# A two-block fp32 model on one core: elementwise work of GpSimd moved to VectorE and ScalarE, and the modulation spread over three feed-forward stages

## The chip, the core and the metric

The kernel runs on one core of one Trainium2 chip. The time is the device time of one execution in microseconds (us). Before the change three runs gave 3841.25 us as the median (3839.11 to 3844.32). TensorE (PE in the profile) multiplies matrices, VectorE (DVE), ScalarE (ACT) and GpSimd (POOL) do the elementwise work, and SyncE (SP) issues the DMA transfers. PEld is the part of TensorE that loads stationary operands.

## The reference, cut to what matters

Two blocks of two layers each, on 512 positions and 1024 channels, all in float32.

```python
# first block, layer i = 0, 1
h = rmsnorm(x, norm_mix[i]); proj = h @ w_in[i]       # state-space scan beside causal attention
x = x + concatenate([y_ssm, y_att]) @ w_out[i]
x = x + memory_attention(rmsnorm(x, norm_mem_q[i]), rmsnorm(mem, norm_mem_kv[i]), ...)
x = x + conv_glu_ffn(rmsnorm(x, norm_ffn[i]), w_up[i], ffn_conv_w[i], ffn_conv_b[i], w_down[i])
# second block, on x and on a context of 256 positions
mod   = silu(c)     @ w_mod[i] + b_mod[i]             # 6 x 1024 numbers: shift, scale, gate, twice
mod_c = silu(c_ctx) @ w_mod[i] + b_mod[i]             # the same for the context
h  = rmsnorm_2(x, g_attn[i]) * (1 + sc1) + sh1        # layer 0: neighbourhood attention
x  = x + gt1 * (o @ w_out)                            # layer 1: sliding window, with rotary positions
x  = x + gt2 * conv_ffn(modulated x, ...)
if i == 0: ctx = ctx + gt1c * (...) ; ctx = ctx + gt2c * conv_ffn(modulated ctx, ...)
```

In layer 1 the context needs only its first shift and scale, since it is not updated there any more.

## The kernel before, in words

Activations lie transposed: channels on the 128 partitions, positions along a row, so `x` is 8 tiles of 128x512. Every float32 product runs as three matmuls on split operands: a tile is rounded by ScalarE to a high part (`hi`) and VectorE subtracts it from the tile to get the low part (`lo`). `wload` (L319) does this for weights: SP loads a tile `wr` of 128x1024 numbers, ScalarE writes `wh` (L314), and another engine writes `wl` (L331). There are 2 buffers of `wr` and 3 each of `wh` and `wl`. `lin` (L304 is its matmul) multiplies high by high, high by low and low by high for each of 8 blocks of 128 channels: 24 matmuls of 512 columns for one weight tile.

The stages follow each other: for each layer of the first block the mixer, the memory attention (`mem_attn`) and the feed-forward (`ffn1`); then for the second block the context and projections (`na_ctx`), the neighbourhood attention (`na_layer`), the feed-forward on both streams (`ffn2`, layer 0), the sliding-window layer (`swa_layer`) and the feed-forward on `x` alone (`ffn2`, layer 1). One feed-forward has 22 pairs of up tiles, in parts, each part followed by its down products into `x`; in `ffn1` the downs of a part are spread over the ups of the next one. Behind each up product of `ffn1` VectorE scales it out of PSUM (L1178), makes two convolution taps (L1183) and, per pair, a gate product (L1186) and a split (L317); in `ffn2` the taps are L2025 and L2027.

GpSimd had these parts of the work. `wload` gave it one weight remainder of three in the first block's mixers, and some later (`WPC`, `WPU`). `sumsq` (L421) made most squares (L429) and nearly all sums of squares (L433) for the norms. The modulation, a matrix-vector product, is made by `mod_steps` (L1246) without TensorE: each of 96 half-rows of weights (one 128x512 load, 256 KB) is multiplied by a broadcast vector, for `x` and for the context, and summed along the row. Six of eight such products ran on GpSimd (L1284) and were summed by ScalarE (L1262, an `accum_out`), two of eight ran on VectorE with the sum in the same instruction (L1282). The steps of layer i were called from the last loop of `mem_attn` and from `ffn1` of the same layer i. GpSimd also had one of two softmax scalings of `na_layer` (L1694), head norms (L1399) and the rotation (L1771, L1762).

Instructions are issued to each engine by a scheduler that looks at the order of the code and at the tiles' readiness; each engine then takes its own in that order, one after another. `issue_after` puts an instruction behind the last matmul issued.

Of the kernel before, what the change touches and what calls it, by code (L numbers as in the profile page):

```python
# [57 lines left out]
HP = (0,1,0)  # L58
# [200 lines left out]
class Builder:  # L259
    def __init__(self, ctx, tc, a, stop=None):  # L260
        self.tc, self.nc, self.a, self.stop = tc, tc.nc, a, stop
        self.n = 0
# [260 lines left out]
    def mixer(self, i, f, fn):  # L523
# [91 lines left out]
        def group_scan(g, conv, zs, fill):  # L615
# [58 lines left out]
            for hp in range(2):  # L674
# [12 lines left out]
        def kv_in(m):  # L687
# [376 lines left out]
    def mem_attn(self, i, f, mh, K, fn):  # L1064
# [1159 lines left out]
```

## Time and profile before

| | |
|---|---|
| median of three runs | 3841.25 us |
| the profiled execution | 3832.78 us, its span 3831.0 us |
| PE, PEld busy | 3675.2 us (96%), 3062.5 us (80%) |
| DVE, ACT, POOL busy | 2669.1 us (70%), 1842.9 us (48%), 1001.0 us (26%) |
| DMA | 354.39 MB, mean 93 GB/s |

A busy time is the union of an engine's instruction times. A busy PE is not a PE at its peak, since matmuls overlap each other and their ends are modelled; the number of matmuls in a stretch tells more. The trace places the stages (us from the start of the span): `ffn1` of layer 0 from about 690 to 1070 and of layer 1 from about 1740 to 2130; `na_ctx` to 2395, `na_layer` to 2605, `ffn2` of layer 0 to 3170, `swa_layer` to 3450, `ffn2` of layer 1 to the end.

### The profile page before, as it was taken

How to read it: one execution, taken by the hardware profiler on the slowest of the kernel's cores; microseconds unless marked ns; L12 is line 12 of the kernel's file. 1: busy time of each engine (PE TensorE's matmuls, PEld its weight loads, DVE VectorE, ACT ScalarE, POOL GpSimd, SP SyncE). 2: the span in 40 equal slices, each digit the busy share in tenths (PEclk: the TensorE clock that was granted, in tenths of full speed). 3: DMA queues.
4: the chain of work that ended last, by engine and by line, in shares of the span. 5: the costliest groups of instructions: out<-in, count | busy, mean ns of one | idle time of the engine just before them, and what ended most of it. 6: DMA issues, size and time to landing. Idle time of an engine off the chain costs nothing. (4 is left out here: it accounts for less than half of the span.)

```text
span 3831.0 us, 55553 instructions
## 1 busy us (share of the span) xinstructions
PE 3675.2 (96%) x21300; PEld 3062.5 (80%) x21300; DVE 2669.1 (70%) x4599; ACT 1842.9 (48%) x3532; POOL 1001.0 (26%) x688
## 2 busy tenths in 40 slices
PE   8999999999899999999999899899999999999999
PEld 6777788777778777887777899778888888888887
DVE  7768756889977687668998753777545547657555
ACT  5645634455555456344555454774222225554232
POOL 1223243467621121234666212321000012100000
PEclk9999999999999999999999999999999999999999
DMA  3222143344422211333444332322212212012232
GB/s 112 67 72 67 51 127 100 111 154 157 146 91 72 72 57 56 126 105 102 165 155 150 123 104 92 108 73 72 66 61 61 66 56 74 15 40 93 94 95 93
DMA packets 128714, 354.39 MB, mean 93 GB/s; under 512 B 14144, under 2 KB 26816, under 8 KB 128448
## 3 DMA queue, kind: packets, MB, share of 16 engines
q1 hardware_dynamic: 127440, 349.62, 28.6%
q8 instruction: 168, 2.75, 0.3%
q10 hardware_dynamic: 1008, 1.21, 0.1%
q14 instruction: 98, 0.80, 0.1%
HBM read 346.58 MB, written 4.19 MB: 92 GB/s over the span
## 5 line engine op out<-in xcount | busy, mean ns | idle before, releaser
L304 PE MATMUL L<-A,wh 128*128 128x512 f32 (+1 forms) x6408 | 1861.5, 375 | 19.5 <-ACT wh L314 8.8
L304 PEld LDWEIGHTS L<-A,wh 128*128 128x128 f32 x6408 | 1148.0, 189 | 241.7 <-ACT wh L314 13.1
L304 PE MATMUL L<-A,wl 128*128 128x512 f32 (+1 forms) x3204 | 1194.9, 373 | 20.4 <-DVE wl L331 19.8
L314 ACT ACTIVATE wh<-wr 128x1024 fp32r<-128x1024 f32 (+4 forms) x562 | 561.9, 1001 | 787.7 <-PE L L304 429.8
L331 DVE TENSOR_TENSOR wl<-wr,wh 128x1024 fp32r<-128x1024 f32 (+4 forms) x503 | 658.7, 1311 | 327.2 <-ACT wh L314 319.1
L304 PEld LDWEIGHTS L<-A,wl 128*128 128x128 f32 x3204 | 604.7, 189 | 137.5 <-DVE wl L331 26.3
L1284 POOL TENSOR_TENSOR A<-A,A 128x512 f32<-128x512 f32 x288 | 482.3, 1706 | 280.6 <-DMA A<-in_w_mod 169.2
L304 PE MATMUL S<-A,wh 128*128 128x512 f32 (+1 forms) x944 | 301.0, 400 | 25.6 <-ACT wh L314 14.7
L331 POOL TENSOR_TENSOR wl<-wr,wh 128x1024 fp32r<-128x1024 f32 (+1 forms) x59 | 139.4, 2363 | 547.4 <-ACT wh L314 473.4
L304 PE MATMUL L<-wh,A 128*128 128x256 f32 x1440 | 272.7, 285 | 2.3 <-ACT A L1309 2.0
L304 PE MATMUL PT<-A,wh 128*128 128x512 f32 (+1 forms) x904 | 262.1, 375 | 0.0
L304 PEld LDWEIGHTS S<-A,wh 128*128 128x128 f32 x944 | 180.9, 195 | 70.8 <-ACT wh L314 16.5
L1183 DVE SCALAR_TENSOR_TENSOR A<-A,vec,A 128x512 f32<-128x512 f32 x176 | 215.2, 1223 | 30.6 <-ACT A L1181 26.4
L304 PEld LDWEIGHTS L<-wh,A 128*128 128x128 f32 x1440 | 226.0, 189 | 8.1 <-issue 4.2
L304 PE MATMUL O<-A,A 128*64 128x128 f32 (+3 forms) x2528 | 228.1, 288 | 4.2 <-DVE A L648 3.6
L433 POOL TENSOR_TENSOR acc<-acc,A 128x512 f32<-128x512 f32 (+1 forms) x44 | 53.8, 1222 | 672.1 <-ACT A L427 670.2
L304 PE MATMUL L<-wl,A 128*128 128x256 f32 x720 | 204.6, 284 | 4.6 <-DVE wl L331 4.6
L304 PEld LDWEIGHTS O<-A,A 128*64 128x64 f32 (+1 forms) x2528 | 168.5, 143 | 48.6 <-issue 24.0
L304 PE MATMUL S<-A,wl 128*128 128x512 f32 (+1 forms) x472 | 189.8, 402 | 17.8 <-DVE wl L331 17.6
L1262 ACT ACTIVATE A<-A 128x512 f32<-128x512 f32 x288 | 177.3, 618 | 38.5 <-POOL A L1284 38.3
L304 PEld LDWEIGHTS PT<-A,wh 128*128 128x128 f32 x904 | 166.7, 191 | 32.7
L314 ACT ACTIVATE A<-A 128x512 fp32r<-128x512 f32 (+2 forms) x202 | 115.3, 571 | 147.4 <-DVE A L1186 78.1
(323 smaller groups left out, 5249.7 us busy)
## 6 DMA issues: line engine op xcount, KB each, us to landing
wr<-in_w_up SPq DMA_DIRECT2D x176, 512.0 KB
A<-in_w_mod SPq DMA_DIRECT2D x192, 256.0 KB
wr<-in_w_qkv SPq DMA_DIRECT2D x62, 512.0 KB
wr<-in_w_in SPq DMA_DIRECT2D x60, 512.0 KB
wr<-in_w_down SPq DMA_DIRECT2D x32, 448.0 KB
wr<-in_w_down SPq DMA_DIRECT2D x32, 384.0 KB
wr<-in_w_down SPq DMA_DIRECT2D x32, 320.0 KB
wr<-in_w_os SPq DMA_DIRECT2D x16, 512.0 KB
```

Of the source, the lines that this page charges most:

```text
L304: self.last_mm = self.nc.tensor.matmul(out, lhsT=l, rhs=r, start=start, stop=stop, skip_group_check=True)
L314: self.nc.scalar.activation(h, src, AF.Copy)
L331: eng.tensor_sub(out=l[:, :cols], in0=r[:, :cols], in1=h[:, :cols].bitcast(F32))
L433: self.mark_p = (add or nc.gpsimd).tensor_add(out=acc.t, in0=acc.t, in1=dst)
L1183: ve.scalar_tensor_tensor(out=ac, in0=u[:, tap:tap + S], scalar=cw(tap), in1=ac, op0=ALU.mult, op1=ALU.add)
L1262: nc.scalar.activation(t, t, AF.Copy, accum_out=o)
L1284: nc.gpsimd.tensor_mul(out=t, in0=w, in1=cv[2 * v + e])
```

## The change

GpSimd keeps the clearing of bias tiles in `na_layer` and the first square and three sums of the kernel; all else goes. Weight remainders, sums of squares, head norms, the softmax scaling and the rotation go to VectorE. Squares go to ScalarE. Every product of the modulation goes to VectorE with its sum in the same instruction. The modulation is also cut otherwise: a step is now one half-row with both vectors, the first 24 of 48 rows of layer 0 are made in `mem_attn` and `ffn1` of layer 0, the other 24 in those of layer 1, and all 48 rows of layer 1 in `ffn2` of layer 0; for the context in layer 1 only 16 rows of 48 are made. Loads of its weights run 2 ahead instead of 4. `ffn2` of layer 0 has four parts instead of three and takes its PSUM banks in turn from three pools instead of one.

```diff
-F1_MOD = (2, 5, 5, 5)
+F1_MOD = (1, 2.5, 2.5, 2.5)
+F2_PARTS = ((0, 6), (6, 6), (12, 5), (17, 5))
+F2_MOD = (0.7, 1.2)
-MSTEP = (0,1,4,1,2)
+MSTEP = (0,0.5)
-MPF = 4
+MPF = 2
...
         self.hi(h[:, :cols], r[:, :cols])
-        self.lo_n += 1
-        if pool is None:
-            pool = self.wp and self.lo_n % self.wp == 0
-        eng = nc.gpsimd if pool else nc.vector
-        eng.tensor_sub(out=l[:, :cols], in0=r[:, :cols], in1=h[:, :cols].bitcast(F32))
+        self.lo(l[:, :cols], r[:, :cols], h[:, :cols])
...
-        if act:
+        if pool[0]:
+            nc.gpsimd.tensor_mul(out=dst, in0=src, in1=src)
+        else:
             nc.scalar.activation(dst, src, AF.Square)
-        else:
-            nc.gpsimd.tensor_mul(out=dst, in0=src, in1=src)
...
-            self.mark_p = (add or nc.gpsimd).tensor_add(out=acc.t, in0=acc.t, in1=dst)
+            (nc.gpsimd if pool[1] else nc.vector).tensor_add(out=acc.t, in0=acc.t, in1=dst)
...
-        self.steps = self.mod_steps(i, 0, 96)
+        self.steps = self.mod_steps(0, 24 * i, 24 * i + 24)
...
-            for v in range(2):
-                t = self.t("A", [P, 512])
-                self.modn += 1
-                o = part[:, v, e, m:m + 1]
-                if self.modn % 8 in MODV:
-                    nc.vector.scalar_tensor_tensor(out=t, in0=w, scalar=1.0, in1=cv[2 * v + e], op0=ALU.mult, op1=ALU.mult, accum_out=o)
-                else:
-                    nc.gpsimd.tensor_mul(out=t, in0=w, in1=cv[2 * v + e])
-                    late.append((o, t))
-            add(MLAG)
-            yield
...
+            for m in range(m0, m1):
+                load(m + MPF)
+                w = ws.pop(m)
+                for v in range(nv(m)):
+                    t = self.t("A", [P, 512])
+                    nc.vector.scalar_tensor_tensor(out=t, in0=w, scalar=1.0, in1=cv[v], op0=ALU.mult, op1=ALU.mult,
+                                                   accum_out=part[:, v, e, m:m + 1])
+                yield
...
-                    (nc.gpsimd if e in NPL else ve).tensor_scalar(out=o.pr[e], in0=o.pr[e], scalar1=o.st[:, 4 + e:5 + e], scalar2=1.0, op0=ALU.mult, op1=ALU.mult)
+                    ve.tensor_scalar(out=o.pr[e], in0=o.pr[e], scalar1=o.st[:, 4 + e:5 + e], scalar2=1.0, op0=ALU.mult, op1=ALU.mult)
...
+        bank = self.next_bank if both else lambda: self.p("L")
+        fparts = F2_PARTS if both else FF_PARTS
+        if both:
+            self.bank = 0
+            self.steps = self.mod_steps(1, 0, 48)
...
                     for s in sorted(streams, reverse=True):
                         up(j, e, s)
+                        if both and j < j0 + nj - 1:
+                            self.step(4 * j + 2 * e + 1 - s, F2_MOD[0])
...
                 down(m, s)
+                if both:
+                    self.step(n, F2_MOD[1] if pi < 3 else 100)
```

How this moves instructions shows best in three places. The lines are those of each kernel, and what follows the arrow is what the instruction reads. First VectorE in `ffn1` of layer 0, between the tenth gate product and the eleventh; before, with L1282 the products of the modulation, L1178 the scaling out of PSUM, L1183 the taps and L331 the weight remainders:

```order
L1282 SCALAR_TENSOR_TENSOR A_7436,mparts<-A_7294,A_5947 128x512
L1282 SCALAR_TENSOR_TENSOR A_7451,mparts<-A_7309,A_5947 128x512
L1282 SCALAR_TENSOR_TENSOR A_7466,mparts<-A_7432,A_5947 128x512
L1177 MEMSET A_7526 128x2
L1178 TENSOR_TENSOR A_7526<-L_7495,rs_6308 128x512
L1177 MEMSET A_7564 128x2
L1183 SCALAR_TENSOR_TENSOR A_7529<-A_7526,vec,A_7529 128x512 x2
L331 TENSOR_TENSOR wl_7644<-wr_7642,wh_7643 128x1024
L1178 TENSOR_TENSOR A_7564<-S_7533,rs_6308 128x512
L331 TENSOR_TENSOR wl_7682<-wr_7680,wh_7681 128x1024
```

and now, where L1262, L1167, L1172 and L310 are the same four:

```order
L1262 SCALAR_TENSOR_TENSOR A_7287,mparts<-A_7165,A_5938 128x512
L1262 SCALAR_TENSOR_TENSOR A_7289,mparts<-A_7165,A_5941 128x512
L1262 SCALAR_TENSOR_TENSOR A_7293,mparts<-A_7279,A_5938 128x512
L1262 SCALAR_TENSOR_TENSOR A_7295,mparts<-A_7279,A_5941 128x512
L1166 MEMSET A_7354 128x2
L1167 TENSOR_TENSOR A_7354<-L_7323,rs_6280 128x512
L310 TENSOR_TENSOR wl_7446<-wr_7444,wh_7445 128x1024
L1172 SCALAR_TENSOR_TENSOR A_7357<-A_7354,vec,A_7357 128x512
L1166 MEMSET A_7392 128x2
L1172 SCALAR_TENSOR_TENSOR A_7357<-A_7354,vec,A_7357 128x512
L1167 TENSOR_TENSOR A_7392<-S_7361,rs_6280 128x512
L310 TENSOR_TENSOR wl_7484<-wr_7482,wh_7483 128x1024
```

Two more products stand ahead of these four, so that VectorE has a run of six here where it had three; the scaling and both weight remainders of the next pair stand behind the run in either kernel, and one weight remainder has moved ahead of the taps. Second, GpSimd in the same stage, before (each a product of the modulation, ten of them in a row about this place):

```order
L1284 TENSOR_TENSOR A_6945<-A_6749,A_5899 128x512
L1284 TENSOR_TENSOR A_6947<-A_6749,A_5944 128x512
L1284 TENSOR_TENSOR A_6953<-A_6757,A_5902 128x512
L1284 TENSOR_TENSOR A_6960<-A_6846,A_5899 128x512
L1284 TENSOR_TENSOR A_6962<-A_6846,A_5944 128x512
```

and now, the end of what GpSimd does in the first mixer (L416 and L422, the square and three sums) and its next instruction, the clearing of a bias tile in `na_layer` (L1628):

```order
L416 TENSOR_TENSOR acc_115<-x 128x512
L422 TENSOR_TENSOR acc_115<-acc_115,A_237 128x512
L422 TENSOR_TENSOR acc_115<-acc_115,A_240 128x512
L422 TENSOR_TENSOR acc_115<-acc_115,A_243 128x512
L1628 MEMSET A_21188 128x256
```

Between those two places GpSimd has no instruction any more: nothing of it lies in either `ffn1`. Third, VectorE in the up products of `ffn2`, layer 0, before, with L2025 and L2027 the taps, L2033 the gate product and L317 its split:

```order
L331 TENSOR_TENSOR wl_26829<-wr_26827,wh_26828 128x1024
L2025 TENSOR_SCALAR A_26657<-A_26653,vec 128x512
L317 TENSOR_TENSOR A_26663<-A_26552,A_26663 128x256
L2027 SCALAR_TENSOR_TENSOR A_26657<-A_26653,vec,A_26657 128x512 x2
L2033 TENSOR_TENSOR A_26585<-A_26585,A_26657 128x512
L317 TENSOR_TENSOR A_26669<-A_26585,A_26668 128x512
```

and now, the same steps as L310, L2006, L2008, L2014:

```order
L310 TENSOR_TENSOR wl_26071<-wr_26069,wh_26070 128x1024
L2006 TENSOR_SCALAR A_25887<-A_25883,vec 128x512
L1262 SCALAR_TENSOR_TENSOR A_25893,mparts<-A_25811,A_24135 128x512
L2008 SCALAR_TENSOR_TENSOR A_25887<-A_25883,vec,A_25887 128x512
L310 TENSOR_TENSOR A_25897<-A_25774,A_25897 128x256
L2008 SCALAR_TENSOR_TENSOR A_25887<-A_25883,vec,A_25887 128x512
L2014 TENSOR_TENSOR A_25807<-A_25807,A_25887 128x512
L310 TENSOR_TENSOR A_25903<-A_25807,A_25902 128x512
```

A product of the modulation stands between the taps, behind the weight remainder and ahead of the gate product.

## Rows read from the trace of the kernel before

**Rows 1.** The page's part 1: busy time, share of the span, instructions

```profile
PE 3675.2 (96%) x21300; PEld 3062.5 (80%) x21300; DVE 2669.1 (70%) x4599; ACT 1842.9 (48%) x3532; POOL 1001.0 (26%) x688
```

**Rows 2.** Stretches: length, busy PE PEld DVE ACT POOL (instructions), PE clock, DMA share, GB/s

```profile
630.00:700.00 70.00, 61.89 (x261) 49.51 (x260) 43.52 (x60) 28.00 (x45) 49.17 (x32) 0.95 0.33 113
700.00:1055.00 355.00, 334.53 (x1403) 266.28 (x1402) 320.51 (x399) 199.86 (x421) 217.79 (x129) 0.98 0.46 148
1055.00:1680.00 625.00, 611.30 (x3551) 495.36 (x3550) 447.38 (x808) 320.14 (x622) 119.32 (x71) 1.00 0.25 77
1680.00:1745.00 65.00, 59.20 (x243) 47.59 (x242) 43.67 (x48) 27.03 (x44) 44.85 (x30) 0.92 0.36 122
1745.00:2105.00 360.00, 338.90 (x1420) 270.44 (x1419) 322.45 (x401) 199.55 (x423) 217.60 (x129) 0.97 0.45 148
2105.00:2240.00 135.00, 124.24 (x891) 115.21 (x890) 101.54 (x187) 73.61 (x120) 21.95 (x13) 0.96 0.42 134
2395.00:2500.00 105.00, 90.36 (x743) 78.88 (x744) 79.01 (x179) 78.67 (x162) 32.41 (x56) 0.93 0.37 109
2500.00:2605.00 105.00, 98.80 (x743) 79.81 (x742) 81.63 (x184) 71.64 (x152) 33.02 (x45) 1.00 0.24 74
2640.00:3140.00 500.00, 499.12 (x2836) 434.75 (x2835) 276.85 (x599) 142.38 (x236) 6.85 (x6) 1.00 0.21 63
3639.00:3735.00 96.00, 96.00 (x416) 77.62 (x415) 54.73 (x89) 28.85 (x38) 0.00 (x0) 1.00 0.31 94
```

**Rows 3.** What PE waits for in 700 to 1055: us, times, longest us

```profile
PE S L304 <- DVE wl L331: 8.1, 4, 3.6
PE L L304 <- DVE wl L331: 7.5, 5, 3.0
```

**Rows 4.** DVE in order of time in 872 to 877: start, us

```profile
872.33 0.68 DVE L1282 SCALAR_TENSOR_TENSOR A<-A,A 128x512 f32<-128x512 f32 x1
...
874.64 1.76 DVE L1282 SCALAR_TENSOR_TENSOR A<-A,A 128x512 f32<-128x512 f32 x1
...
876.35 0.68 DVE L1178 TENSOR_TENSOR A<-L,rs 128x512 f32<-128x512 f32 x1
```

**Rows 5.** POOL in order of time in the same stretch

```profile
872.48 8.04 POOL L1284 TENSOR_TENSOR A<-A,A 128x512 f32<-128x512 f32 x5 [1.49 <-DVE A L317]
```

**Rows 6.** DVE groups in 700 to 1055: count, busy us, mean ns, idle before

```profile
L1183 DVE SCALAR_TENSOR_TENSOR A<-A,vec,A 128x512 f32<-128x512 f32 x85 | 103.7, 1220 | 14.0 <-ACT A L1181 12.4 <-issue 0.2
L331 DVE TENSOR_TENSOR wl<-wr,wh 128x1024 fp32r<-128x1024 f32 x39 | 60.4, 1549 | 10.5 <-ACT wh L314 10.5
L1282 DVE SCALAR_TENSOR_TENSOR A<-A,A 128x512 f32<-128x512 f32 x45 | 57.2, 1295 | 0.0
...
L1282 DVE DVE_READ_ACCUMULATOR A<-A,A 128x1 f32 x45 | 3.5, 79 | 0.0
```

**Rows 7.** DVE groups in 2640 to 3140

```profile
L2027 DVE SCALAR_TENSOR_TENSOR A<-A,vec,A 128x512 f32<-128x512 f32 x84 | 62.9, 749 | 1.3
L331 DVE TENSOR_TENSOR wl<-wr,wh 128x1024 fp32r<-128x1024 f32 x47 | 57.6, 1226 | 68.7 <-ACT wh L314 67.7
```

**Rows 8.** POOL groups of the whole span

```profile
L1284 POOL TENSOR_TENSOR A<-A,A 128x512 f32<-128x512 f32 x288 | 482.3, 1706 | 280.6 <-DMA A<-in_w_mod 169.2 <-ACT A L1262 50.2 <-DVE A L317 23.9
L331 POOL TENSOR_TENSOR wl<-wr,wh 128x1024 fp32r<-128x1024 f32 x54 | 132.8, 2459 | 525.1 <-ACT wh L314 451.0 <-PE O L304 30.8 <-PE PT L1596 16.6
...
L1694 POOL TENSOR_SCALAR A<-A,sm 128x512 f32<-128x512 f32 x32 | 28.7, 896 | 90.3 <-DVE sm L1692 72.5 <-DMA A<-d 7.6 <-PE PT L1697 5.2
```

**Rows 9.** DVE group of the whole span, line 1694

```profile
L1694 DVE TENSOR_SCALAR A<-A,sm 128x512 f32<-128x512 f32 x32 | 17.3, 541 | 0.8
```

**Rows 10.** ACT groups in 700 to 1055

```profile
L1262 ACT ACTIVATE A<-A 128x512 f32<-128x512 f32 x135 | 83.0, 617 | 1.7 <-POOL A L1284 1.7
...
L1262 ACT ACTIVATION_READ_ACCUMULATOR A<-A 128x1 f32 x135 | 25.1, 186 | 0.0
```

**Rows 11.** The page's part 6: DMA issues, count, KB each

```profile
A<-in_w_mod SPq DMA_DIRECT2D x192, 256.0 KB
```

More of the change, by code (lines that the diff above doesn't have):

```diff
@@ L57 @@
 HB = 1
-HP = (0,1,0)
 MC = (2,2)
@@ L419, in new_acc, with sumsq @@
         return acc
-    def sumsq(self, acc, src, first, last=False, act=True, add=None, key="", tag=None):
+    def sumsq(self, acc, src, first, last=False, pool=(False, False), key="", tag=None):
         nc = self.nc
@@ L737, in mixer @@
         V = []
-        wv = [self.wload(a[f"w_uv{i}"][hf], pool=False) for hf in range(2)]
+        wv = [self.wload(a[f"w_uv{i}"][hf]) for hf in range(2)]
         for tb in range(4):
@@ L1147, in mem_attn, with next_bank @@
             self.step(m, MSTEP[1])
+    def next_bank(self):
+        self.bank += 1
+        return self.p(FTAGS[self.bank % len(FTAGS)])
     def step(self, n, r):
@@ L1243, in mod_prep, with mod_steps @@
         self.G = [[self.c([P, KD, 2], name=f"G{i}{j}") for j in range(2)] for i in range(DEPTH)]
-    def mod_steps(self, i, n0, n1):
+    def mod_steps(self, i, m0, m1):
         nc = self.nc
-        cv = []
-        for v in range(2):
-            for e in range(2):
+        part = self.mparts
+        nv = lambda m: 2 if i < DEPTH - 1 or m < 16 else 1
+        for e in range(2):
+            cv = []
+            for v in range(2):
                 c = self.t("A", [P, 512])
@@ L1254, in mod_steps @@
                 cv.append(c)
-            yield
-        part = self.mparts
-        late = []
-        def add(k):
-            while len(late) > k:
-                o, t = late.pop(0)
-                nc.scalar.activation(t, t, AF.Copy, accum_out=o)
-        ws = {}
-        def load(n):
-            if n < n1:
-                ws[n] = self.t("A", [P, 512])
-                nc.sync.dma_start(out=ws[n], in_=self.a["w_mod"][i, n // 2, n % 2])
-        for n in range(n0, n0 + MPF):
-            load(n)
@@ L1288, in mod_steps, with load @@
-        add(0)
-        if n1 == 96:
-            for v in range(2):
-                mo = self.mod[i][:, :, v]
-                nc.vector.tensor_add(out=mo, in0=part[:, v, 0], in1=part[:, v, 1])
-                nc.vector.tensor_add(out=mo, in0=mo, in1=self.v(f"b_mod{i}"))
+            ws = {}
+            def load(m):
+                if m < m1:
+                    ws[m] = self.t("A", [P, 512])
+                    nc.sync.dma_start(out=ws[m], in_=self.a["w_mod"][i, m, e])
+            for m in range(m0, m0 + MPF):
+                load(m)
@@ L1558, in x_qk @@
             for j in range(4):
-                h.norm(j, nc.gpsimd)
+                h.norm(j, nc.vector)
             self.xtok[g] = h.raw
@@ L2034, in gate @@
             return self.split(A)
-        for pi, (j0, nj) in enumerate(FF_PARTS):
+        for pi, (j0, nj) in enumerate(fparts):
             act = {s: [] for s in streams}
-            last = pi == len(FF_PARTS) - 1
+            last = pi == len(fparts) - 1
             first = 0
```

72 lines of the change are left out of this document (28 added, 44 removed).

## The prediction, made before the changed kernel was run

> **What bounds the kernel now.** I read the page's busy times first, then the stretches stage by stage, then what TensorE waits for, and last VectorE's instructions by form in two stages. TensorE is busy 96% of the span [rows 1], so all its idle time is 156 us: no change that leaves the matmuls alone can win more than some 5%. Where is the loss? The reader is to look in [rows 2] at TensorE's count of matmuls in two stretches of the same kind of work. In the last feed-forward, 3639 to 3735, TensorE passes 416 matmuls in 96 us, 0.2308 us each, with VectorE busy 57% and GpSimd at rest. In the two `ffn1` stretches it passes 1403 in 355 us and 1420 in 360 us, 0.253 us each. At 0.2308 us they would take 323.8 and 327.7 us: 31.2 and 32.3 us are lost there, 63.5 together, the largest loss of any stage. The granted clock is 0.98 and 0.97 in them and 1.00 in the reference stretch, so a part of the loss is the lower of the clock's two levels (1.2 and 2.4 GHz) after TensorE had idled; it goes when the idling goes.
>
> TensorE's two largest waits there are for `wl`, VectorE's weight remainder, 8.1 and 7.5 us [rows 3]. VectorE is 90% busy (320.5 of 355). Why so busy is seen in the order of time: a product of the modulation takes 0.68 us when GpSimd rests and 1.76 us when GpSimd's own products run without a pause beside it, while the scaling out of PSUM takes 0.68 us in the midst of them [rows 4, 5]. So the two engines take turns at something that an instruction with two SBUF operands needs. By form the reader sees the same: the taps average 1.220 us in `ffn1` against 0.749 in `ffn2`, the remainder 1.549 against 1.226 [rows 6, 7].
>
> A choice lies here. By TensorE's busy time only 20.5 and 21.1 us are idle in the two stretches, 41.6 together [rows 2]. The Trainium skill (Perfetto Trace Analysis, "Identifying the Most-Contended Engine") says that matmul busy time is a poor measure of how near TensorE is to its limit, because matmuls are pipelined, and names the busy share of weight loads instead. By it the stretches have 266.28/355 and 270.44/360, 75.0 and 75.1%, against 77.62/96 = 80.9% at 3639, which would put the loss at 51.5 us. The trace agrees that busy time understates it. I take neither but the count of matmuls, 63.5 us; by busy time all gains in `ffn1` below would be a third smaller, and the forecast some 16 us higher.
>
> **The change part by part.** *`ffn1`, both layers.* GpSimd's 129 products in each (217.8 us of its time) go, and with them VectorE's turns: 85 taps x (1.220 - 0.749) = 40.0, 39 remainders x (1.549 - 1.226) = 12.6, 45 products x (1.295 - 0.68) = 27.7, in all 80.3 us off VectorE [rows 4, 6, 7]. Its 45 products become 88 (96 for the half of layer 0, less 8 made in `mem_attn`): 43 more x (0.68 + 0.079 for the accumulator read) = 32.6 us [rows 4, 6]. VectorE comes to 320.5 - 80.3 + 32.6 = 273 us in a stretch whose matmuls need 324 us. ScalarE is rid of 83.0 + 25.1 us of row sums [rows 10]. VectorE's share is then about 82%. How much loss is left at 82%? The nearest rows are 1055 to 1680 (72% VectorE, TensorE idle 13.7 of 625, 2.2%) and `ffn1` now (90%). I take 2.2% of 652 us, 14 us, because a remainder that isn't held up costs TensorE nothing while three buffers of `wl` stand ahead; a run of six products (4.6 us) is shorter than the 24 matmuls of one weight tile (5.5 us). Gain 63.5 - 14 = 49 us; bounds 32 (half regained) and 63 (all).
>
> *The starts of `ffn1`* (630 to 700, 1680 to 1745). TensorE idles 8.1 and 5.8 us; GpSimd is busy 49.2 of 70 and 44.9 of 65 us with sums of squares and the first products, and the norm waits for these sums [rows 2]. They go to VectorE, squares to ScalarE, and the products from 16 to 8 (the steps of the code). Half of 13.9: gain 7, bounds 0 and 14.
>
> *2105 to 2240*, the end of `ffn1` of layer 1 and the context's norm: TensorE idles 10.8 us, GpSimd is busy 22. Gain 3, bounds 0 and 10.
>
> *Mixers and `mem_attn`.* 54 remainders go from 2.46 us on GpSimd to 1.23 on VectorE [rows 7, 8]; the sums come too, and the turns go. GpSimd works 119 us in 1055 to 1680; at the ratio 1.226/2.459 that is at most 60 us for VectorE, less the squares, which go to ScalarE, and less the turns: I take VectorE's 72% as unchanged. TensorE idles 13.7 us there. Gain 2, bounds -10 and 14.
>
> *`na_layer`* (2395 to 2605). Here VectorE takes more than it sheds: GpSimd works 65.4 us, of which scalings go from 0.896 to 0.541 us and the rest to about half [rows 2, 8, 9]: some 33 us more for VectorE, less about 8 us of turns (a guess from its few long instructions), on 160.6 of 210. From 76 to 88%, and TensorE, which idles 20.8 us there, depends on short chains. Loss 6, bounds a loss of 21 (idling doubled) and a gain of 10.
>
> *`ffn2`, layer 0.* TensorE idles 0.9 of 500 us with VectorE at 55% (276.9 us) [rows 2]. It takes 128 products x 0.76 = 97 us, and a fourth part adds 16 accumulations into `x` and the context, at most 0.749 us each, 12 us: about 102 us of the 109 fall into these 500, 76%. The cover is TensorE itself, at 0.2308 us a matmul; if VectorE falls behind, its weight remainders are late. Transfers: 96 of 192 loads of 256 KB come here [rows 11], 25 MB over 535 us, 47 GB/s on top of 63; `ffn1` carried 148 without the queue as the wait. Loss 3, bounds 0 and 45 (the slow rival). `swa_layer`: rotation and head norms go to VectorE; loss 1, bounds -5 and 3.
>
> Sum: 49 + 7 + 3 + 2 - 6 - 3 - 1 = 51 us. The profiled execution took 3832.8 us, 8.5 below the median of 3841.25; less 51 it is 3782, and on the median's footing **3790 us**.
>
> **The rivals.** *More.* Every stage that had GpSimd beside VectorE sheds most of its idling: `ffn1` 60, the starts 12, 2105 to 2240 8, mixers 10, `na_layer` 5: 95 us, 3746 us. For it: idle time sits where GpSimd works, and there is nearly none from 2640 to 3140 [rows 2]. Against it: at 1055 to 1680 TensorE idles only 2.2% though GpSimd works.
> *Less.* The runs of six products stand ahead of both remainders and of the scaling that frees a PSUM bank, and the same waits for `wl` come back at 82%: `ffn1` regains 32, `na_layer` loses 15, `ffn2` 5: 12 us, 3829 us. For it: VectorE works in order and 0.85 of its former load remains (273 of 320.5).
> *Slower.* One mechanism, in `ffn2` of layer 0: VectorE's queue there becomes what `ffn1`'s was. The products and extra accumulations put remainders late, TensorE idles and its clock falls: at `ffn1`'s rate of loss (32.3/360, 9%) 500 us lose 45. `na_layer` doubles its 20.8, and `ffn1` regains only 32: -34, 3875 us. It decides from the point where the products in front of a remainder last longer than two weight tiles of TensorE's work, 11 us, since three buffers stand ready. Against it: the products are laid singly between taps there, and VectorE's 76% is near the 72% that lost 2.2%.
> *Nothing.* VectorE's total stays about the same (320 products, remainders and sums come, turns go), and if TensorE's waits come from the chain load, `wh`, `wl` rather than from turns, what leaves `ffn1` returns elsewhere: 3841 us. Against it: the waits in `ffn1` name `wl` by VectorE, not `wh` or the load [rows 3].
>
> **How the numbers follow.** My forecast has 0.57 (3765 to 3815), More 0.15, Less 0.15, Nothing 0.06, Slower 0.07. Two thirds of More and most of Less belong in the range: 3740 to 3836. No change is within 0.2%, 7.7 us, about what a measurement of this kernel can tell: 3833.6 to 3848.9. Faster: forecast, More and nearly all of Less, 0.85; same: Nothing and the end of Less, 0.07; slower 0.08.
>
> **What would show it.** In `ffn1`: taps at 0.75 us, products at 0.68, matmuls at 0.2308 us or at most 0.236, clock 1.00; VectorE about 80% busy. In `ffn2` of layer 0: VectorE near 76% and TensorE idle by a few us of 535. In `na_layer`: VectorE near 88% and the stage some 6 us longer. I am wrong if taps stay above 1 us without GpSimd (the turns were another's doing), if matmuls stay near 0.25 us in `ffn1` though VectorE has room, or if `ffn2` of layer 0 grows by over 10 us.

## The result, and the profile after

The changed kernel takes 3718.36 us (median of four runs, 3717.45 to 3722.77); the kernel before took 3840.18 us on the same chip (four runs, 3837.0 to 3844.32). The ratio is 0.9684, 95% interval 0.9668 to 0.9701: 122 us gained where 51 were forecast, and below the range's lower end of 3740. The profiled execution took 3722.77 us with a span of 3721.0, 110.0 us less than the profiled one before; the other 12 lie in where the two stand to their medians (7.4 below, 4.4 above).

The page's part 1 of the kernel after, against [rows 1]: TensorE's idle time falls from 156 to 72 us, VectorE is a little less busy with 735 instructions more, and GpSimd is at rest.

```profile
PE 3649.1 (98%) x21300; PEld 3053.3 (82%) x21300; DVE 2618.1 (70%) x5334; ACT 1705.5 (46%) x3042; POOL 21.0 (1%) x56
```

The stretches after that answer to those of [rows 2], and ahead of them the first stretch of layer 0's mixer, and its mixer and `mem_attn` as a whole (columns as there). They are cut where TensorE has begun as many matmuls as at the ends of the stretches before.

```profile
0.00:53.50 53.50, 42.94 (x179) 32.98 (x180) 40.62 (x85) 31.12 (x40) 5.63 (x8) 1.00 0.42 148
0.00:607.00 607.00, 590.16 (x3434) 477.84 (x3435) 422.98 (x860) 337.72 (x659) 5.63 (x8) 0.99 0.26 83
607.00:666.00 59.00, 58.72 (x262) 47.64 (x261) 38.23 (x79) 24.80 (x33) 0.00 (x0) 1.00 0.36 119
666.00:991.00 325.00, 325.00 (x1402) 262.91 (x1401) 253.86 (x478) 120.44 (x153) 0.00 (x0) 1.00 0.40 129
991.00:1604.00 613.00, 608.99 (x3550) 495.72 (x3549) 424.64 (x845) 336.16 (x653) 0.00 (x0) 1.00 0.25 78
1604.00:1659.00 55.00, 54.97 (x246) 44.54 (x245) 35.41 (x65) 24.56 (x33) 0.00 (x0) 1.00 0.38 125
1659.00:1988.00 329.00, 329.00 (x1418) 265.80 (x1417) 258.96 (x491) 123.42 (x159) 0.00 (x0) 1.00 0.41 131
...
2274.00:2381.00 107.00, 90.25 (x739) 78.19 (x737) 86.76 (x201) 76.84 (x159) 8.06 (x27) 0.94 0.35 106
2381.00:2492.00 111.00, 102.28 (x746) 82.90 (x745) 88.54 (x212) 72.61 (x154) 5.55 (x16) 0.97 0.22 67
2525.00:3024.00 499.00, 498.69 (x2836) 434.19 (x2835) 359.79 (x887) 143.81 (x244) 0.00 (x0) 1.00 0.36 115
```

Both `ffn1` now run 0.232 us a matmul (325/1402, 329/1418) at clock 1.00, with VectorE 78 and 79% busy; the list of TensorE's waits has no row left for 666 to 991, where [rows 3] named `wl`. `ffn2` of layer 0 took 128 products in and passes its 2836 matmuls in 499 us instead of 500.

VectorE's groups in 666 to 991 (count, busy us, mean ns, idle before), which answer to [rows 6]: L1172 are the taps, L1262 the products of the modulation, L310 the weight remainder.

```profile
L1172 DVE SCALAR_TENSOR_TENSOR A<-A,vec,A 128x512 f32<-128x512 f32 x85 | 63.7, 749 | 7.0 <-ACT A L1170 5.4
L1262 DVE SCALAR_TENSOR_TENSOR A<-A,A 128x512 f32<-128x512 f32 x88 | 56.0, 688 | 0.5 <-DMA A<-in_w_mod 0.5
L310 DVE TENSOR_TENSOR wl<-wr,wh 128x1024 fp32r<-128x1024 f32 x39 | 47.7, 1224 | 11.0 <-ACT wh L307 11.0
```

The same three forms fall from 1220 to 749, from 1295 to 688 and from 1549 to 1224 ns. Two of a run of four products in order of time, against [rows 4]:

```profile
819.99 0.69 DVE L1262 SCALAR_TENSOR_TENSOR A<-A,A 128x512 f32<-128x512 f32 x1
820.60 0.08 DVE L1262 DVE_READ_ACCUMULATOR A<-A,A 128x1 f32 x1
820.60 0.69 DVE L1262 SCALAR_TENSOR_TENSOR A<-A,A 128x512 f32<-128x512 f32 x1
```

The accumulator read does not even hold the next product up: products start 0.61 us apart.

Where the 110 us come from, by the stretches of before. I worked this table out from the traces, which hold the same 21300 matmuls: the length of a stretch before less the time in which the other kernel passes the same matmuls. Its last rows are experiments told of below.

| us gained in | 0:630 | 630:700 | 700:1055 | 1055:1680 | 1680:1745 | 1745:2105 | 2105:2395 | 2395:2605 | 2605:3140 | 3140:3470 | to the end |
|---|---|---|---|---|---|---|---|---|---|---|---|
| stage | mixer 0 | start | ffn1, 0 | mixer 1 | start | ffn1, 1 | na_ctx | na_layer | ffn2, 0 | swa | ffn2, 1 |
| forecast | 2 with mixer 1 | 7, both | 49, both | | | | 3 | -6 | -3 | -1 | 0 |
| after | 22.8 | 11.3 | 29.7 | 11.8 | 10.7 | 30.4 | 4.6 | -8.8 | 3.3 | -6.5 | 0.6 |
| e1, modulation alone | -1.4 | 11.2 | 30.9 | -1.4 | 10.6 | 32.1 | 4.0 | -2.9 | 4.8 | -3.7 | 0.9 |
| e2, remainders alone | 18.8 | 0.3 | -0.6 | 1.4 | 0.1 | 1.5 | -1.1 | -1.2 | -0.7 | 2.0 | 0.3 |
| e3, squares and sums alone | 11.4 | 9.1 | -0.6 | 7.4 | 9.7 | 0.9 | 2.7 | -3.9 | 1.3 | -1.2 | 0.3 |
| e4, the rest alone | 0.7 | -1.5 | 0.8 | -3.6 | 0.0 | 0.1 | -4.4 | -7.4 | 1.1 | -4.2 | 0.6 |
| e7, products to VectorE, old places | -2.9 | 9.8 | 30.2 | -3.7 | 10.7 | 31.9 | -3.3 | -2.5 | 1.0 | -0.7 | 1.5 |
| e8, new places, GpSimd kept | -1.1 | 3.8 | 30.9 | -1.2 | 6.0 | 30.3 | 4.8 | -2.0 | -17.2 | -2.1 | 1.4 |

("Mixer" includes `mem_attn`.) The reader should see three sources: `ffn1` 60.1, mixers and `mem_attn` 34.6, the starts of `ffn1` 22.0.

### The profile page after: what moved, and what is told of

It reads as the page before. It is cut to its first block, busy times and chain, and to the rows that moved or that the text cites. A ratio compares the mean times of both kernels' runs of the same rounds, so it can differ in the third digit from the quotient of the medians.

```text
span 3721.0 us, 54589 instructions
## 1 busy us (share of the span) xinstructions
PE 3649.1 (98%) x21300; PEld 3053.3 (82%) x21300; DVE 2618.1 (70%) x5334; ACT 1705.5 (46%) x3042; POOL 21.0 (1%) x56
## 3 DMA queue, kind: packets, MB, share of 16 engines
q1 hardware_dynamic: 129168, 350.67, 29.7%
## 5 line engine op out<-in xcount | busy, mean ns | idle before, releaser
L297 PE MATMUL L<-A,wh 128*128 128x512 f32 (+1 forms) x5060 | 1516.9, 382 | 15.2 <-DVE x L1919 4.6
L297 PEld LDWEIGHTS L<-A,wh 128*128 128x128 f32 x5060 | 913.9, 189 | 200.7 <-issue 9.8
L297 PE MATMUL L<-A,wl 128*128 128x512 f32 (+1 forms) x2530 | 960.5, 380 | 2.1 <-DVE wl L310 2.0
L310 DVE TENSOR_TENSOR wl<-wr,wh 128x1024 fp32r<-128x1024 f32 (+4 forms) x570 | 649.6, 1140 | 283.0 <-ACT wh L307 249.6
L297 PE MATMUL S<-A,wh 128*128 128x512 f32 (+1 forms) x1592 | 462.1, 373 | 10.1 <-ACT wh L307 8.7
L297 PE MATMUL PT<-A,wh 128*128 128x512 f32 (+1 forms) x1604 | 435.1, 358 | 0.0
L297 PE MATMUL PT<-A,wl 128*128 128x512 f32 (+1 forms) x802 | 287.1, 358 | 2.7 <-DVE wl L310 2.7
L1262 DVE SCALAR_TENSOR_TENSOR A<-A,A 128x512 f32<-128x512 f32 x320 | 207.0, 687 | 10.7 <-DMA A<-in_w_mod 8.9
L297 PEld LDWEIGHTS O<-A,A 128*64 128x64 f32 (+1 forms) x2528 | 170.0, 143 | 46.8 <-issue 25.9
L2008 DVE SCALAR_TENSOR_TENSOR A<-A,vec,A 128x512 f32<-128x512 f32 (+1 forms) x264 | 173.7, 662 | 5.0
L297 PEld LDWEIGHTS PT<-A,wl 128*128 128x128 f32 x802 | 151.5, 189 | 27.0 <-DVE wl L310 3.1
L297 PE MATMUL S<-A,A 128*128 128x256 f32 (+4 forms) x832 | 151.8, 314 | 10.6 <-DVE sm L1660 5.5
```

The costliest lines, as they stand in the source:

```text
L297: self.last_mm = self.nc.tensor.matmul(out, lhsT=l, rhs=r, start=start, stop=stop, skip_group_check=True)
L310: self.nc.vector.tensor_sub(out=l, in0=src, in1=h.bitcast(F32))
L1262: nc.vector.scalar_tensor_tensor(out=t, in0=w, scalar=1.0, in1=cv[v], op0=ALU.mult, op1=ALU.mult, accum_out=part[:, v, e, m:m + 1])
L2008: ve.scalar_tensor_tensor(out=ac, in0=u[:, tap:tap + n], scalar=cw(tap), in1=ac, op0=ALU.mult, op1=ALU.add)
```

## The experiments

My theory: GpSimd's two-operand instructions and VectorE's take turns, so VectorE's work in front of `wl` becomes late, and wherever the pair stops TensorE's idling stops. The rival: it is the load and the place, that is, `ffn1` simply had too much modulation in it, and who makes it matters little. A second question was where the 70 us beyond the forecast come from. Ratios are to the kernel before, timed on the same chip, with the 95% interval.

| | median, us | ratio |
|---|---|---|
| e1_mod_only | 3747.39 | 0.976 (0.9746 to 0.9775) |
| e2_wl_only | 3812.72 | 0.9925 (0.9909 to 0.9941) |
| e3_sq_only | 3800.68 | 0.9899 (0.9883 to 0.9916) |
| e4_rest_only | 3849.24 | 1.0028 (1.0017 to 1.0039) |
| e5_idle_two | 3871.16 | 1.0101 (1.0082 to 1.012) |
| e6_idle_one | 3720.13 | 0.9702 (0.9687 to 0.9717) |
| e7_mod_here | 3760.94 | 0.9812 (0.9796 to 0.9827) |
| e8_mod_place | 3780.52 | 0.9863 (0.9848 to 0.9879) |
| e9_after_again | 3717.86 | 0.9681 (0.9667 to 0.9694) |
| e10_na_back | 3714.65 | 0.967 (0.9657 to 0.9683) |
| e11_swa_back | 3713.82 | 0.9669 (0.9656 to 0.9682) |
| e12_all_back | 3711.01 | 0.9662 (0.9649 to 0.9675) |

### One part of the change at a time (e1 to e4)

**e1_mod_only**: before, with the new modulation (steps, places, `ffn2` of layer 0 with four parts and three banks) and, beside it, one of 59 weight remainders moved from GpSimd to VectorE.

```diff
-F1_MOD = (2, 5, 5, 5)
+F1_MOD = (1, 2.5, 2.5, 2.5)
+F2_MOD = (0.7, 1.2)
...
-        self.steps = self.mod_steps(i, 0, 96)
+        self.steps = self.mod_steps(0, 24 * i, 24 * i + 24)
```

> The kernel before with the modulation part of the change alone: all its products on VectorE, spread over three feed-forwards, and the four parts and bank order of ffn2. Theory A (turns: what costs time is that GpSimd's two-operand instructions and VectorE's take turns, wherever they meet): both ffn1 stretches come to 0.231 us a matmul, 60 us off, the starts of ffn1 keep the sums of squares on GpSimd and lose half of their 22 us; 3840 becomes about 3770. Theory B (load and place: what counts is that 108 us of ScalarE and half of the products left each ffn1; the other moves come to nothing): the whole gain of 122 us is here, 3718 to 3725.

90 us, where theory A had said some 70: the part is worth three quarters of the whole. It wins all of `ffn1` (63.0 us, against the 63.5 lost there by the count of matmuls), and also both starts (21.8) though the sums of squares stay on GpSimd.

**e2_wl_only**: before, with every weight remainder on VectorE.

```diff
-        if pool is None:
-            pool = self.wp and self.lo_n % self.wp == 0
+        pool = False
```

> The kernel before with all weight remainders on VectorE, nothing else. A: 139 us of GpSimd time go, 34 of the 59 remainders lie in layer 0's mixer and memory attention: 10 to 20 us faster, nearly all between 0 and 630, about 3825. B: VectorE gets 72 us more in stretches where it is 72 to 76% busy: no change or up to 5 us slower, 3840 to 3845.

25 us, nearly all of it in the mixer and `mem_attn` of layer 0.

**e3_sq_only**: before, with the squares on ScalarE and the sums on VectorE (all but the first square and three sums, as in the changed kernel).

```diff
-        if act:
+        if act or key:
...
-            self.mark_p = (add or nc.gpsimd).tensor_add(out=acc.t, in0=acc.t, in1=dst)
+            self.mark_p = (nc.gpsimd if tag == 'A' and add is None else nc.vector).tensor_add(out=acc.t, in0=acc.t, in1=dst)
```

> The kernel before with squares on ScalarE and sums of squares on VectorE, nothing else. A: some 250 us of GpSimd time go, much of it in the mixers and just ahead of ffn1, where the norm waits for the sum: 15 to 25 us faster, 8 to 12 of it at the two starts of ffn1, about 3820. B: no change, 3835 to 3845, since VectorE gets 79 us more.

37 us: half of it in the two starts (18.8), half in the mixers (18.8).

**e4_rest_only**: before, with the softmax scaling, head norms and rotation on VectorE.

```diff
-NPL = (1,)
+NPL = ()
...
-                h.norm(j, nc.gpsimd)
+                h.norm(j, nc.vector)
...
-            eng = nc.gpsimd
+            eng = ve
```

> The kernel before with softmax scalings, head norms and rotation on VectorE, nothing else. A and B: slower by about 10 us, 3850, because na_layer and the sliding-window layer have short chains in which VectorE gets more work (they lost 8.8 and 9 us in the changed kernel). If this is no slower, the loss there comes from the remainders or from the sums.

This part loses 11 us, most of it in `na_ctx`, `na_layer` and `swa_layer`. The four parts gain 90 + 25 + 37 - 11 = 141 us, the whole 122: they overlap. The starts are won by e1 alone and by e3 alone, some 20 us counted twice.

Why either is enough shows in GpSimd's order of time before, at the start of `ffn1` of layer 0: the sums of squares (L433), a weight remainder (L331) and the products (L1284) stand in one queue.

```profile
651.53 2.85 POOL L331 TENSOR_TENSOR wl<-wr,wh 128x1024 fp32r<-128x1024 f32 x1
...
670.13 2.02 POOL L429 TENSOR_TENSOR sq<-x 128x512 f32<-128x512 f32 x1 [1.91 <-DVE x L1145]
672.22 1.62 POOL L433 TENSOR_TENSOR acc<-acc,sq 128x512 f32<-128x512 f32 x1
673.80 2.55 POOL L1284 TENSOR_TENSOR A<-A,A 128x512 f32<-128x512 f32 x2
676.29 1.06 POOL L429 TENSOR_TENSOR sq<-x 128x512 f32<-128x512 f32 x1
677.43 1.27 POOL L433 TENSOR_TENSOR acc<-acc,sq 128x512 f32<-128x512 f32 x1
```

The last square starts right behind two products, and the norm behind the last sum. What TensorE waits for there, before and then after:

```profile
PE O L304 <- DVE rt L379: 3.3, 1, 3.3
PE S L304 <- ACT A L437: 2.5, 1, 2.5
PE S L304 <- DVE A L438: 2.3, 1, 2.3
```

```profile
PE O L297 <- DVE rt L368: 0.3, 1, 0.3
```

### Turns, or load and place (e5 to e8)

**e5_idle_two**: after, with 132 products on GpSimd in each `ffn1` that nobody reads.

```diff
+                for _ in range(6):
+                    with self.after(PIN):
+                        nc.gpsimd.tensor_mul(out=self.junk, in0=p.act[-1][0].bitcast(F32), in1=self.rope)
```

**e6_idle_one**: the same with one operand read.

```diff
+                        nc.gpsimd.tensor_scalar(out=self.junk, in0=p.act[-1][0].bitcast(F32), scalar1=2.0, scalar2=None, op0=ALU.mult)
```

(Both have one buffer fewer for activations, 58, to make room for the output.)

> The changed kernel, and in each ffn1 132 more products on GpSimd (two SBUF operands, 128x512) that nothing reads, six behind each pair of up products; the pool of work tiles has one buffer less to make room. Theory A (turns): VectorE's taps go from 0.749 back to about 1.2 us, its busy time in ffn1 from 254 to some 330 us, past the matmuls' 325, and each ffn1 gets 15 to 30 us longer: 3718 becomes 3750 to 3780. Theory B (load and place): GpSimd's work is on no path, so no change, 3716 to 3725.

> As the run with 132 unread products in each ffn1, but with one SBUF operand (a product with a constant). A, if turns are taken by whole instructions of GpSimd: VectorE waits less since these take about 0.9 us instead of 1.7, taps near 1.0 us, 3718 becomes 3725 to 3745. A, if only GpSimd's second operand disturbs: taps stay 0.75 us, 3718. B: 3718.

e5 takes 151 us longer than e6, timed beside it, and is slower than the kernel before, by more than theory A had said (3750 to 3780); e6 stands 2 us from the changed kernel in the median (ratios 0.9702 and 0.9684, their intervals overlap). Stretch 700 to 980 of e5, its two VectorE groups that answer to [rows 6] (L1267 the products, L310 the gate's split), GpSimd's group, and TensorE's waits:

```profile
700.00:980.00 280.00, 246.41 (x992) 193.50 (x991) 262.62 (x338) 85.86 (x109) 147.61 (x91) 0.95 0.33 108
```

```profile
L1267 DVE SCALAR_TENSOR_TENSOR A<-A,A 128x512 f32<-128x512 f32 x63 | 99.9, 1631 | 0.0
...
L310 DVE TENSOR_TENSOR A<-A,A 128x512 fp32r<-128x512 f32 x15 | 25.7, 1713 | 0.7 <-ACT A L307 0.7
```

```profile
L1202 POOL TENSOR_TENSOR junk<-A,rope 128x512 f32<-128x512 f32 x91 | 149.2, 1640 | 132.5 <-ACT A L307 126.5
```

```profile
PE L L297 <- DVE wl L310: 15.3, 6, 4.3
PE S L297 <- DVE wl L310: 6.0, 3, 2.8
PE PT L297 <- DVE wl L310: 4.8, 3, 2.5
```

And of e6, the same stretch, products and GpSimd:

```profile
700.00:980.00 280.00, 280.00 (x1207) 226.41 (x1206) 247.99 (x417) 102.47 (x129) 175.45 (x108) 1.00 0.39 129
```

```profile
L1267 DVE SCALAR_TENSOR_TENSOR A<-A,A 128x512 f32<-128x512 f32 x80 | 66.2, 875 | 0.7 <-DMA A<-in_w_mod 0.7
```

```profile
L1202 POOL TENSOR_SCALAR junk<-A 128x512 f32<-128x512 f32 x108 | 175.5, 1625 | 104.4 <-ACT A L307 96.9
```

GpSimd's instruction lasts about the same in both (1640 and 1625 ns), and VectorE has the same instructions to do. Only in e5 do its products take 1.63 us, `wl` come late and the matmuls fall to 992 in 280 us. So neither more modulation nor its place is needed for the loss, and the rival in its plain form falls. GpSimd's instructions of one operand slow VectorE too (VectorE's products take 875 ns in e6 and 688 in the changed kernel), but TensorE is not held up: it is busy in all 280 us. In order of time e5 shows the end of GpSimd's run at 826.6 us as a step in VectorE:

```profile
825.42 1.74 DVE L1267 SCALAR_TENSOR_TENSOR A<-A,A 128x512 f32<-128x512 f32 x1
827.10 0.07 DVE L1267 DVE_READ_ACCUMULATOR A<-A,A 128x1 f32 x1
827.10 0.68 DVE L1267 SCALAR_TENSOR_TENSOR A<-A,A 128x512 f32<-128x512 f32 x1
```

**e7_mod_here**: before, with all products on VectorE at their old places, so that each `ffn1` has twice the products of the changed kernel.

```diff
-                if self.modn % 8 in MODV:
+                if True:
```

**e8_mod_place**: the places of e1, but six of eight products still on GpSimd, summed by ScalarE.

```diff
+                    if self.modn % 8 in MODV:
+                        nc.vector.scalar_tensor_tensor(out=t, in0=w, scalar=1.0, in1=cv[v], op0=ALU.mult, op1=ALU.mult, accum_out=o)
+                    else:
+                        nc.gpsimd.tensor_mul(out=t, in0=w, in1=cv[v])
+                        late.append((o, t))
```

> The kernel before with all products of the modulation on VectorE, with the sum in the instruction, and their number and place unchanged: 192 in each layer's mem_attn and ffn1. A: VectorE sheds its turns (80 us) and takes 134 more products at 0.76 us: 320 - 80 + 102 = 342 us against 324 of matmuls, so each ffn1 is bound by VectorE at some 345 us and gains about 10; the starts gain 8 each: 3840 becomes about 3805. If the place didn't matter (engine alone), the gain would be that of the modulation part alone, 90 us, 3750.

> The modulation part of the change with its new places (half a layer in each ffn1, layer 1 in ffn2 of layer 0), but with six of eight products on GpSimd and summed by ScalarE, as before. A: in ffn1 half the turns stay, VectorE at about 320 - 40 - 17 = 263 us has room, so each ffn1 gains 20 to 28; ffn2 of layer 0 gets 96 turns and loses up to 10: 3840 becomes 3785 to 3800. If it is the engine and not the place that counts, 3830 or slower.

Against e1's 90 us the engine alone (e7) is worth 75 and the place alone (e8) 55. Either wins `ffn1` whole, which theory A had not expected: it gave e7 some 10 us for each `ffn1`, since at 0.76 us a product VectorE would have 342 us of work, and e8 20 to 28. What the place alone loses is half of the starts and, in `ffn2` of layer 0, where GpSimd now works beside VectorE, 17.2 us. So of the rival this much stays: fewer products of the old kind in `ffn1` would have done for `ffn1`, but the loss moves with them. e7's stretch in `ffn1` and its products:

```profile
700.00:1030.00 330.00, 328.48 (x1418) 265.77 (x1417) 305.01 (x663) 120.69 (x153) 3.41 (x3) 1.00 0.48 158
```

```profile
L1282 DVE SCALAR_TENSOR_TENSOR A<-A,A 128x512 f32<-128x512 f32 x176 | 109.6, 686 | 0.0
```

VectorE is busy 305 of 330 us, 92%, more than before the change (90%), and TensorE loses almost nothing (330 us for 1418 matmuls, 0.2327 each), though the products stand in runs of up to ten there. e8's stretch in `ffn1` has the turns and yet no loss: GpSimd works 98.6 of 323 us on products and VectorE's own take 1.16 us each, but they are few, and TensorE is never idle.

```profile
698.00:1021.00 323.00, 323.00 (x1398) 262.31 (x1397) 244.17 (x344) 160.49 (x285) 98.55 (x63) 1.00 0.39 129
```

And e8 in `ffn2` of layer 0, where the products are slow again:

```profile
2580.00:3090.00 510.00, 495.67 (x2780) 431.20 (x2779) 338.98 (x673) 201.20 (x428) 145.64 (x100) 0.98 0.34 110
```

```profile
L1288 DVE SCALAR_TENSOR_TENSOR A<-A,A 128x512 f32<-128x512 f32 x32 | 34.5, 1081 | 5.0 <-DMA A<-in_w_mod 2.8 <-POOL A L1290 1.9 <-ACT A L1261 0.2
```

TensorE's longest waits there name ScalarE, which sums GpSimd's products in this kernel:

```profile
PE S L306 <- ACT A L316: 4.6, 1, 4.6
PE S L306 <- ACT wh L316: 3.5, 1, 3.5
PE PT L306 <- ACT A L316: 3.0, 1, 3.0
```

How much of the 17 us is ScalarE's and how much the turns' was not told apart.

### What GpSimd was good for (e9 to e12)

**e9_after_again** is the changed kernel once more, without an edit, as the base of the next three, timed beside them. **e10_na_back** gives one of two softmax scalings back to GpSimd, **e11_swa_back** the rotation, its tables and the head norms of `swa_layer`, and **e12_all_back** both and the head norms of the context's queries and keys.

```diff
-                    ve.tensor_scalar(out=o.pr[e], in0=o.pr[e], scalar1=o.st[:, 4 + e:5 + e], scalar2=1.0, op0=ALU.mult, op1=ALU.mult)
+                    (nc.gpsimd if e else ve).tensor_scalar(out=o.pr[e], in0=o.pr[e], scalar1=o.st[:, 4 + e:5 + e], scalar2=1.0, op0=ALU.mult, op1=ALU.mult)
```

```diff
-                ve.tensor_mul(out=v(z)[:, :, :, d], in0=v(x)[:, :, :, o], in1=tb(1, d))
+                nc.gpsimd.tensor_mul(out=v(z)[:, :, :, d], in0=v(x)[:, :, :, o], in1=tb(1, d))
...
-                h.norm(t2, nc.vector, y[t2])
+                h.norm(t2, nc.gpsimd, y[t2])
```

> The changed kernel once more, as the measure for the other runs on this chip: 0.968 of the time before, about 3716 to 3720.

> The changed kernel with the second softmax scaling of each unit of na_layer back on GpSimd: 32 instructions with one SBUF operand. Theory A as it stands now (GpSimd's two-operand instructions make VectorE wait, one-operand ones hardly): VectorE is rid of 17 us there without turns, na_layer gets 3 to 8 us shorter, 3712. Rival (the 8.8 us lost in na_layer come from remainders and sums, which stay on VectorE): no change, 3718.

> The changed kernel with rotation, its tables and the head norms of the sliding-window layer back on GpSimd: 34 two-operand instructions, 0.9 to 1.1 us each. A: they are few, and VectorE has 26% idle there, so the layer regains 2 to 5 of the 6.5 us it lost: 3714. Rival (it lost them to something else, as to the order of issue): no change, 3718.

> The changed kernel with softmax scaling, rotation and all head norms of the second block back on GpSimd, which is everything that the run with these alone on VectorE showed as a loss (11 us). A: 6 to 12 us faster than the changed kernel, 3706 to 3712. Rival: within 3 us of it.

In the table's measure `na_layer` stands at -6.5 in e9 and at -2.4 in e10, `swa_layer` at -6.6 in e9 and at -1.7 in e11: both lose less with GpSimd's help, by 4.1 and 4.9 us. e12 is the fastest of all, 6.9 us below e9; the intervals of the two ratios still touch (0.9667 to 0.9675), while their runs do not (3708.2 to 3714.49 against 3714.99 to 3722.25). Single stretches of two traces of the same kernel differ by up to 3 us here (mixer 0: 22.8 and 25.9), so e10 and e11, 3 and 4 us from e9, are told by their stage and not by their time, and even there not by much.

## Why the prediction was wrong, point by point

The direction was right, and so was the mechanism for `ffn1`, the turns. The sum was not: -51 forecast, -122 measured, with the measured time outside the range. Three terms failed: the mixers with `mem_attn` (2 forecast, 34.6 measured), whose bounds were read in one of two layers; the starts of `ffn1` (7 and 22.0), taken by half of the idle time; and the residue left in `ffn1` (14 of 63.5, measured 3.4).

**Turns (right).** Taps were forecast at 0.75 us and came out at 0.749, products 0.68 and 0.688, matmuls at most 0.236 us and 0.232, clock 1.00. VectorE came to 253.9 us in 325, 78%, where 273 and "about 80%" stood: the sum left out the gate's splits and the smaller remainders, which got 16.3 us shorter by the same groups (18.4 to 15.1, 24.0 to 15.3, 12.5 to 8.2). e5 and e6 show the turns as the cause of VectorE's long instructions, and not only beside them. The Trainium skill (GPSIMD Engine Reference, "1. Specifications") says that GpSimd shares its SBUF interfaces with VectorE and contends with VectorE's instructions that have two SBUF inputs. The trace agrees: 1.77 us against 0.68 for the same product in e5, and 0.68 for a scaling whose source is in PSUM [rows 4].

**`ffn1` (term +49, measured +60.1).** The loss of 63.5 us by the count of matmuls was the right measure: more was regained than weight loads (51.5) or idle time (41.6) would have allowed. What failed is the residue of 14 us, put in by VectorE's share of the time. At a share of 92% in e7 hardly 3 us are left of 330. What goes with the loss in `ffn1` is VectorE's work against what the same matmuls need at 0.2308 us each:

| | VectorE busy, us | matmuls need, us | quotient | stretch over need |
|---|---|---|---|---|
| e5, 700 to 980 | 262.6 | 992 x 0.2308 = 229.0 | 1.15 | 22% |
| before, 700 to 1055 [rows 2] | 320.5 | 323.8 | 0.99 | 9.6% |
| e7, 700 to 1030 | 305.0 | 327.3 | 0.93 | 0.8% |
| e6, 700 to 980 | 248.0 | 278.6 | 0.89 | 0.5% |
| after, 666 to 991 | 253.9 | 323.6 | 0.78 | 0.4% |
| e8, 698 to 1021 | 244.2 | 322.7 | 0.76 | 0.1% |

In these stretches VectorE's queue, with three buffers of `wl` behind it, costs next to nothing until its work nears the need. The last row has turns and no loss: the turns as such cost no time there. No run has VectorE at 0.99 without turns, so how near is too near is not shown. The 2.2% of 1055 to 1680 on which I leaned came mostly of something else: TensorE's idle time there fell from 13.7 to 4.0 us, and of the 11.8 us gained the squares and sums alone (e3) bring 7.4.

**The starts (term +7, bound 14, measured +22.0).** I took half of the idle time, after having argued that idle time understates a loss. By the count of matmuls against 0.2308 us the two starts lost 9.8 and 8.9 us (70 - 261 x 0.2308, 65 - 243 x 0.2308), and clock and idling both recovered: 59 us for 262 matmuls at clock 1.00, which is 0.225 us each, so that 0.2308 is a little too much here and the count too gives less than the 22.0 measured. The step should have been whole and counted: e1 takes the products out of GpSimd's queue and leaves the sums there, e3 the other way round; either ends nearly all of this loss.

**Mixers and `mem_attn` (term +2, bounds -10 and 14, measured +34.6).** The worst step. The term was bounded by the idle time of 1055 to 1680 alone, layer 1. Layer 0's mixer and memory attention, 0 to 630, were not read at all. Before (columns as in [rows 2]), the first stretch and all of it:

```profile
0.00:60.00 60.00, 46.12 (x179) 35.19 (x180) 43.68 (x80) 31.77 (x41) 12.97 (x11) 0.94 0.39 132
0.00:630.00 630.00, 595.02 (x3434) 478.90 (x3435) 434.76 (x797) 330.70 (x633) 168.76 (x103) 0.99 0.26 81
```

TensorE idles 35.0 of these 630 us, and GpSimd is busy 168.8, with 32 of the 54 remainders of [rows 8] and 23 of the 73 sums of squares of the form below among it:

```profile
L331 POOL TENSOR_TENSOR wl<-wr,wh 128x1024 fp32r<-128x1024 f32 x32 | 78.7, 2460 | 289.2 <-ACT wh L314 265.6 <-PE PT L997 16.6 <-PE O L304 6.9
L433 POOL TENSOR_TENSOR acc<-acc,sq 128x512 f32<-128x512 f32 x23 | 38.9, 1689 | 29.7 <-ACT sq L427 28.2
```

e2 and e3 win 18.8 and 11.4 us there, the whole change 22.8. TensorE hardly waits for GpSimd's remainder itself: 0.6 us of its waits in 0 to 630 name it. But a remainder can hold up a short instruction of VectorE for its whole length. At 34.8 us one does so in the chain of the norm, and TensorE then waits 2.1 us for the end of that chain (L379). VectorE's and GpSimd's rows before, and VectorE's same instruction in e2, where GpSimd rests:

```profile
34.83 2.38 DVE L369 TENSOR_SCALAR rt<-rt 128x4 int32<-128x4 int32 x1
```

```profile
34.80 2.38 POOL L331 TENSOR_TENSOR wl<-wr,wh 128x1024 fp32r<-128x1024 f32 x1 [10.21 <-ACT wh L314]
```

```profile
32.44 0.17 DVE L368 TENSOR_SCALAR rt<-rt 128x4 int32<-128x4 int32 x1
```

Eight instructions of VectorE in 0 to 630 that elsewhere take under 0.5 us take 1.28 to 2.44 there, each begun beside a remainder on GpSimd. In 0 to 100 TensorE waits 7.4 us for VectorE's results other than `wl`, and in e2's 0 to 90, for all but 4 of the 416 matmuls, 0.6 us. How much of the 18.8 us the eight explain was not worked out. My assumption that VectorE's share would stay held here too, and was no reason for no gain: it was busy 434.8 of 630 us before and is 423.0 of 607 after, 69 and 70%, but in shorter instructions.

**2105 to 2240 (term +3):** 4.6, up to 2395. **`na_layer` (term -6): -8.8.** Near in size, but not for the reason given: VectorE was to be 88% busy and is 80% (175.3 of 218). TensorE's idle time grew from 20.8 to 25.5 us, 2.9 of it in two waits of the first half, which after, in 2274 to 2381, read

```profile
PE PT L1672 <- DVE A L427: 5.9, 3, 2.5
PE S L297 <- DVE sm L1660: 5.1, 6, 2.2
```

and were 4.4 and 3.7 us on the same two tiles before. In the second half the granted clock fell from 1.00 to 0.97. With the scaling back on GpSimd, which reads one tile, e10 regains 4 against e9. **`swa_layer` (term -1, bounds -5 and 3): -6.5**, of which e11 regains 4.9: mis-sized. TensorE's wait for one split of VectorE is 1.3 us there before, 4.2 after and 1.3 again in e11; which of rotation, tables and head norms made it late was not told apart. **`ffn2`, layer 0 (term -3): +3.3.** VectorE 72% busy, not 76, TensorE idle 0.3 of 499 us.

**The rivals.** *More* (95 us, 3746) came nearest: its reason, that idle time sits where GpSimd works, was the right reading, but it had mixers at 10, the starts at 12 and a chance of 0.15. What stood against it, the 2.2% of 1055 to 1680, was itself mostly part of the gain. *Less* and *Nothing* fall with 60 us in `ffn1`. *Slower* did not come about, and e8 shows its place: `ffn2` of layer 0 loses 17 us when GpSimd keeps the products and ScalarE the sums.

## What to carry to other kernels

When an engine is emptied, list every stage in which it works, from the first microsecond, and put a bound on each by the same measure; a bound read from one stage does not hold for its sister. Judge an engine's queue by its work against what TensorE needs for the same matmuls, not by its share of the time: in `ffn1` 93% of the need cost 0.8% and 99% cost a tenth. That holds for a queue with buffers behind it; `na_layer`, `swa_layer` and e8's `ffn2` lost time with VectorE 66 to 80% busy. GpSimd can still take single instructions of stages with short chains (e10 to e12: 3 to 7 us), with one operand if possible, but not beside long work of VectorE on two-operand tiles, and not long instructions beside a short chain of VectorE.

## What the runs showed of the hardware

That the kind of GpSimd's instruction decides was not expected so sharply. Six two-operand products of GpSimd in a row take 10.30 us in e5, and every two-operand product of VectorE beside them 1.74 to 1.78 us; six one-operand instructions in e6 take about as long (10.20 us), but VectorE's products beside them alternate between 0.68 and 1.08 us:

```profile
803.25 0.68 DVE L1267 SCALAR_TENSOR_TENSOR A<-A,A 128x512 f32<-128x512 f32 x1
803.87 0.07 DVE L1267 DVE_READ_ACCUMULATOR A<-A,A 128x1 f32 x1
803.87 1.08 DVE L1267 SCALAR_TENSOR_TENSOR A<-A,A 128x512 f32<-128x512 f32 x1
```

With 264 instructions of the first kind the kernel takes 151 us longer than with 264 of the second. On VectorE's side it is not the instructions with two operands alone that wait: the 128x4 one at 34.83 us before reads one tile, and takes 2.38 us beside a remainder on GpSimd and 0.17 without.

The Trainium skill (SBUF — State Buffer, "Who interferes with whom") says that the pair of ports which the two engines share is an exclusive lock, and that a VectorE instruction with two SBUF inputs contends with a GpSimd instruction that reads SBUF. That the pair is held for the whole instruction it says of VectorE's two-port modes alone. e5 agrees that they contend, and there it is for about a whole instruction: one product of VectorE (1.70 us from start to start) passes for each of GpSimd's (10.30/6 = 1.72). In e6 they contend as well, but not for so long: two products of VectorE pass (1.63 us from pair to pair) for each of GpSimd's 1.70 us, and the second is held up 0.4 us, much less than GpSimd's instruction lasts.
